# P times V as plain 32-bit matmuls on the two column halves of the array, and output-weight blocks staged in three tiles in turn

## The chip, the cores and the metric

The kernel runs on one core of one Trainium2 chip. The metric is the device time of one execution in microseconds (us), the median of several runs. The core has TensorE (PE), which multiplies a moving tile by a stationary one of up to 128 columns; VectorE (DVE), ScalarE (ACT) and GpSimd (POOL), which work on tiles; and SyncE (SP), whose queue issues the kernel's transfers. PE writes to PSUM, which DVE and ACT read.

## The reference

One layer of a hybrid backbone on 1024 latent tokens and 256 context tokens of width 1024, all in 32-bit floating point. The part that matters here, cut to its core:

```python
# 8 query heads in 2 groups of 4, one key/value head per group, head size 64,
# blocks of 128 queries; keys: the block, its two neighbours, and the context
s_loc = jnp.einsum('bnqhgd,bnkhd->bnhgqk', qb, kw) * scale
s_ctx = jnp.einsum('bnqhgd,bchd->bnhgqc', qb, kc) * scale
m = jnp.maximum(jnp.maximum(s_loc.max(-1), s_ctx.max(-1)), sk)
p_loc = jnp.exp(s_loc - m); p_ctx = jnp.exp(s_ctx - m)
inv = 1.0 / (p_loc.sum(-1) + p_ctx.sum(-1) + jnp.exp(sk - m))
o = (jnp.einsum('bnhgqk,bnkhd->bnqhgd', p_loc * inv, vw)
     + jnp.einsum('bnhgqc,bchd->bnqhgd', p_ctx * inv, vc))
...
mix_x = jnp.concatenate([att_x, ml_x], axis=-1) @ w_out
x = x + gt_m * rms_norm(mix_x, g_post_mix)
fx = swiglu(modulate(rms_norm(x, g_pre_ffn), sh_f, sc_f), w_ffn_in, w_ffn_out)
x = x + gt_f * rms_norm(fx, g_post_ffn)
```

Beside the attention, `ml_x` is a bidirectional mLSTM over chunks of 64 tokens. `att_x` and `ml_x` are 512 wide each; together they meet the output weight `w_out`.

## The kernel before

Most matmuls are split: a 32-bit operand is kept as a rounded part (type fp32r, "hi") and the remainder ("lo"), made by `split` (L64: ACT casts, L65: DVE subtracts), and the product is summed from two or three fp32r matmuls (`mm3`, L76 to L78, three). Plain 32-bit matmuls stand beside these: transposes (against an identity matrix), the mLSTM's L876 and L880, and L704, where the mLSTM's state step puts four matmuls of 64 stationary columns into the two halves of the PSUM partitions in turn.

The attention stage is a loop over 16 items, one for each block n of 128 queries and group g (item i has n = i // 2, g = i % 2). In item i:

- `Soft(i+2)`, for the item two later: scores per head (PE L972, L973), mask, sink and minimum (DVE L974), exponential (ACT L983), normalisation (POOL L988), into the tile `pr` (3 buffers).
- `Values(i)`: `tr(t)` transposes the probabilities of key tile t for four heads (L1002) into a PSUM bank `pt` (3 buffers) and splits them to `th` and `tl`; `mm(t)` multiplies by the values with L1012 (`th`) and L1013 (`tl`). The stationary tile `av2` has hi and lo of V side by side, 64 columns each, so the two halves of the result `po` must still be added: `out` copies one half (ACT L1020) and adds it to the other into `mix` (DVE L1021). A block has five key tiles, the first and the last block four: 76 in all.
- In items 0 to 7 the mLSTM of block i: scores (L862), two passes of values (L876 and L880; ACT L892, DVE L894 into `hs`), norm, output gate and transposes (L910, DVE L911). `hs` is loaded from DRAM by SP (L852).
- The output weight: eight blocks of 128 x 1024, each loaded raw into the one tile `wor` (`wout_raw(i)`, L926), and split at the letter `p` of the same item (ACT L938, POOL L939). `WSPLIT` says which block in which item (items 1, 2, 3, 5, 6, 7, 8, 9). The first three go to the tiles `woxh` and `woxl` and from there to DRAM (L921, in the next item), and are loaded again in items 8 and 9.

The strings `PLAN_ML` (items 0 to 7), `PLAN` (8 to 12) and `PLAN13` write out the order inside an item: T transposes, A scores, N exponentials, M products, O output, V, z, s, x mLSTM, p weight split. A scheduler moves instructions of independent work past each other on this basis; the end of the stage, from item 14 on, is a hand-written order (`manual_schedule`), in which the output projection (`omm`) is mixed with the last two items. The FFN follows.

Of the kernel before, what the change touches and what calls it, by code (L numbers as in the profile page):

```python
# [9 lines left out]
F32 = mybir.dt.float32  # L10
F32R = mybir.dt.float32r
# [3 lines left out]
ADD, SUB, MUL, MAX, MIN = ALU.add, ALU.subtract, ALU.mult, ALU.max, ALU.min  # L15

P = 128
D = 1024
KT = D // P
S = 1024  # L20
NT = S // P
L = 256
NC_ = L // P
# [8 lines left out]
VSIL, VCONV, VGML, VBADA, VGPM, VGPF = 0, 16, 28, 32, 64, 72  # L32
VID = 80
NVEC = VID + P
PLAN_ML = "T0 A0 A1 A2 A3 T1 T2 T3 M0 M1 T4 V0 N0 M2 M3 M4 O z V1 w s N1 x p l"
PLAN = "T0 A0 A1 A2 A3 T1 T2 T3 N0 M0 T4 M1 M2 N1 M3 M4 O z p l"
PLAN13 = "T0 A0 A1 A2 A3 m T1 T2 P0 T3 N0 M0 T4 M1 P1 M2 N1 M3 P2 M4 O P3 l"
WR = ((1, 2), (4, 5), (6, 7), (0, 3), (14, 15), (10, 13), (12, 8), (9, 11))
WTRIP = (3, 6, 7)
WLOADS = {8: (3, 6), 9: (7,)}  # L40
WSPLIT = {1: 3, 2: 6, 3: 7, 5: 0, 6: 4, 7: 1, 8: 2, 9: 5}


def body(tc, x, ctx, vecs, bcv, bada, gqm, gqf, wada, ws1, ws2, wt, wout, wfi, wfo,
         const, cosc, sinc, out):
    nc = tc.nc
    pe, act, dve, pool = nc.tensor, nc.scalar, nc.vector, nc.gpsimd
    dma = nc.sync.dma_start
# [13 lines left out]
    def split(hi, lo, raw):  # L62

        act.copy(hi, raw)  # L64
        dve.tensor_tensor(lo, raw, hi.bitcast(F32), SUB)  # L65
# [73 lines left out]
    vp = open_pool("V")  # L139
    V = vp[1].tile([P, NT, 4, 129], F32, name="V")  # L140
    Vc = vp[1].tile([P, NC_, 4, 129], F32, name="Vc")
    vp[1].tile([P, 88], F32, name="padv")
    av2 = vp[1].tile([P, NT + NC_, 4, 64], F32R, name="av2")
    G = vp[1].tile([P, 4, 16, 4], F32, name="G")
    pool.memset(V[:, :, :, 128:129], 1.0)
    pool.memset(G, 0.0)
# [6 lines left out]
    hl = [htp[1].tile([P, 4, S], F32R, name=f"hl{i}") for i in range(2)]  # L153
# [48 lines left out]
    pts = {}  # L202
# [94 lines left out]
    for sec in (1, 0):  # L297
        pr = [pa.tile([4, 512], F32, name=f"pr{sec}{i}", tag="mm", bufs=4) for i in range(2)]
        for kt in range(KT):
            w = R(8 + kt, f"wa{sec}_{kt}", (D,))  # L300
# [16 lines left out]
            for n, (k, a, b) in enumerate(ops):  # L317
                if late and n < 2:
                    prep_t(1, True, (n,))
                for i in range(2):  # L320
                    r = pe.matmul(pr[i], a[:, k, :], b[:, i * 512:(i + 1) * 512], start=kt == 0 and n == 0,
                                  stop=kt == KT - 1 and n == len(ops) - 1)
# [19 lines left out]
        r = act.copy(r4[:, 0:512], pr[0])  # L342
# [7 lines left out]
        for q in range(2):  # L350
            t = (hcol, scol)[sec][:, q]
# [36 lines left out]
    def vrow(i):  # L388
        return V[:, i] if i < NT else Vc[:, i - NT]

    def s1(i):
        ps = slab(i, 272, w1h, w1l)
        sf = i + 2 if i < NT else i - NT
        sb = 9 - i if i < NT else 1 - (i - NT)
        dve.tensor_tensor(G[:, 0:2, sf, :], ps[:, 0:8].rearrange("p (k h) -> p k h", h=4),
                          bcr[:, 0:8].rearrange("p (k h) -> p k h", h=4), ADD)
        dve.tensor_tensor(G[:, 2:4, sb, :], ps[:, 8:16].rearrange("p (k h) -> p k h", h=4),
                          bcr[:, 8:16].rearrange("p (k h) -> p k h", h=4), ADD)
        split(av2[:, i, 0::3], av2[:, i, 1:3], ps[:, 16:144].rearrange("p (g v) -> p g v", v=64))
        act.copy(vrow(i)[:, 0, 0:128], ps[:, 144:272])  # L400

    NI = NT + NC_
# [19 lines left out]
    for i in range(NI):  # L422
# [7 lines left out]
        if i == 0:  # L430
            r = st[:, 13:14]
# [7 lines left out]
        if i in (1, 2):  # L439
            b = i - 1  # L440
# [138 lines left out]
    def T(i, name):  # L579
        return q2.tile([P, S], F32, name=name, tag=f"s{i}")  # L580
# [134 lines left out]
    NIT = len(items)  # L715
    qhl, prs, wo, qlast = {}, {}, {}, [None]
# [23 lines left out]
    for j, name in enumerate(TILES):  # L740
# [4 lines left out]
        ps = tproj(j, name in ("mk0", "mk1", "ak"))  # L745
        i = int(name[-1]) if name[-1].isdigit() else 0
# [4 lines left out]
        elif name == "ak":  # L751
# [4 lines left out]
            th = T(0, "kth")  # L756
            for a, b, w, dst in ((kr, ks, S, slice(0, S)), (kc[:, 0:L], kc[:, L:2 * L], L, slice(S, S + L))):
                t = th[64:P] if w == S else kc[64:P, 2 * L:3 * L]
# [7 lines left out]
        elif name.startswith("aq"):  # L766
            t = T(0, f"aq{i}")
# [6 lines left out]
        else:  # L774
            t = R(14 if i == 3 else 15, "so", (S,))
# [26 lines left out]
        if 0 <= j - 3 < 9:  # L802
            s_ = j - 3
            if s_ >= 1 and s_ % 2 == 1:
                k = (s_ - 1) // 2
# [9 lines left out]
    pb = psB[1]  # L815
    mixp = open_pool("mix", side="right")
    mixt = mixp[1].tile([P, NT, 8, P], F32, name="mix")
    mix = [mixt[:, n] for n in range(NT)]
    atp = open_pool("att")
    qa = atp[1]  # L820
    for x_ in "hl":
        qa.tile([P, 4, P], F32R, name=f"t{x_}_", tag=f"pt{x_}", bufs=3)
    qa.tile([P, 80], F32, name="padq")
    for x_, n in (("pt", 3), ("po", 1)):
        pb.tile([P, 4, P], F32, name=x_, tag=x_, bufs=n)
# [88 lines left out]
    wraw = {}  # L914

    def wout_raw(i):

        j = WSPLIT.get(i - 1)
        if j in WTRIP:
            for d, t in zip(wo_d, wraw.pop(j)):  # L920
                dma(d[j], t.bitcast(F32))  # L921
        if i in WSPLIT:
            j = WSPLIT[i]
            wraw[j] = qa.tile([P, D], F32, name=f"wor{j}", tag="wor", bufs=1)
            with tc.issue_after(qlast[0]):
                dma(wraw[j], wout[j])  # L926

    def wout_tiles(j):
        return tuple(R(WR[j][p], f"wo{'hl'[p]}{j}", (D,), F32R) for p in range(2))
# [60 lines left out]
    class Values:  # L990
        def __init__(self, i):
            self.n, self.g = items[i]
            self.pr = prs.pop(i)
            self.kb0, _, self.nb = blocks(self.n)
            self.nt = self.nb + 2
            self.po = pb.tile([P, 4, P], F32, name="po", tag="po", bufs=1)
            self.p = {}

        def tr(self, t):
            pt = bank()  # L1000
            for h in range(4):
                pe.transpose(pt[:, h, :], self.pr[:, h, 1 + t * P:1 + (t + 1) * P], ident)  # L1002
            th = qa.tile([P, 4, P], F32R, name="th_", tag="pth", bufs=3)
            tl = qa.tile([P, 4, P], F32R, name="tl_", tag="ptl", bufs=3)
            split(th, tl, pt)
            self.p[t] = th, tl

        def mm(self, t):
            vt = self.kb0 + t if t < self.nb else NT + t - self.nb
            v2 = av2[:, vt, 2 * self.g:2 * self.g + 2].rearrange("p a v -> p (a v)")  # L1010
            th, tl = self.p.pop(t)
            pe.matmul(self.po, v2, th, start=t == 0, stop=False)  # L1012
            pe.matmul(self.po, v2, tl, start=False, stop=t == self.nt - 1)  # L1013

        def out(self):

            g = self.g
            rg, ot = slice(g * 64, g * 64 + 64), slice(64 - g * 64, P - g * 64)
            o2 = qa.tile([P, 4, P], F32, name="o2", tag="o2", bufs=1)
            act.copy(o2[rg], self.po[ot])  # L1020
            dve.tensor_tensor(mix[self.n][rg, 0:4, :], self.po[rg], o2[rg], ADD)  # L1021

    tc.keep_in_program_order(act.preload_act_table_set("natural_log_exp_and_others"))
    ml_load(0)
    for i in range(2):
        a = Soft(i)
# [14 lines left out]
    def omm(n, hf, ks):  # L1041

        h, l = mhl[n, hf]
        first, last = (0, 7) if n == 0 else (4, 3)
        for k in ks:
            j = 4 * hf + k
            for i in range(2):
                sl = slice(i * 512, (i + 1) * 512)
                mm3(ops_[n][:, sl], (h[:, k], l[:, k]), (wo[j][0][:, sl], wo[j][1][:, sl]), j == first, j == last)


    for i in range(NIT):
        a = Soft(i + 2) if i + 2 < NIT else None
        b = Values(i)
        if i + 3 < NIT:
            q_load(i + 3)
        if i == NIT - 2:
            break
        wout_raw(i)
        for k in (PLAN_ML if i < NT else PLAN13 if i == NIT - 3 else PLAN).split():  # L1060
            op, n = k[0], int(k[1:] or 0)
            if op == "w" and i + 1 < NT:
                ml_load(i + 1)
            elif op == "T" and n < b.nt:
                b.tr(n)
            elif op == "M" and n < b.nt:
                b.mm(n)
            elif op == "O":
                b.out()
            elif op == "A" and a:  # L1070
                a.scores(n)
            elif op == "N" and a:
                a.norm(n)
            elif op == "V" and i < NT:
                ml_values(i, n)
            elif op == "x" and i < NT:
                ml_norm(i)
            elif op == "s" and i + 1 < NT:
                ml_scores(i + 1)
            elif op == "z" and 1 <= i <= NT:  # L1080
                ml_out(i - 1)
            elif op == "l":
                for j in WLOADS.get(i, ()):
                    wout_load(j)
            elif op == "p" and i in WSPLIT:
                wout_split(i)
            elif op == "m":
                msplit(0, 0)
                ops_[0] = pb.tile([P, 1024], F32, name="op", tag="s", bufs=2)
            elif op == "P":  # L1090
                omm(0, 0, range(n, n + 1))
# [1 line left out]

    order = tc.manual_schedule()
    order.__enter__()
    def mm_t(b, *ts):
        for t in ts:
            b.mm(t)

    msplit(0, 1)  # L1100
    b.tr(0)
    b.tr(1)
    b.tr(2)
    omm(0, 1, range(1))
    mm_t(b, 0, 1)
    b.tr(3)
    omm(0, 1, range(1, 2))
    mm_t(b, 2, 3)
    b2 = Values(NIT - 1)
    b2.tr(0)  # L1110
    b.out()
    b2.tr(1)
    omm(0, 1, range(2, 3))
    b2.tr(2)
    msplit(1, 1)
    act.preload_act_table_set("sqrt_and_others")
    mm_t(b2, 0, 1)
    b2.tr(3)
    omm(0, 1, range(3, 4))
    mm_t(b2, 2, 3)  # L1120
    ops_[1] = pb.tile([P, 1024], F32, name="op", tag="s", bufs=2)
    omm(1, 1, range(4))
    b2.out()
    order.__exit__(None, None, None)
    close(atp)
    close(aqp)
# [165 lines left out]
    th = {}  # L1292
# [73 lines left out]
    N1 = NT - 1  # L1366
# [359 lines left out]
    for p in range(4, HT):  # L1726
        j = p - 5
# [40 lines left out]
        else:  # L1768
            X4 += two_banks()
            t = pb.tile([P, D], F32, name="fx2", tag="s", bufs=2)  # L1770
# [97 lines left out]
    for s_ in range(1, 8):  # L1868
        q0 = (s_ - 1) * NJ
        KL = 4 if s_ == 7 else 2  # L1870
        if s_ == 2:
            t = pb.tile([P, D], F32, name="fy0", tag="s", bufs=2)
# [120 lines left out]
```

## Time and profile before

| what | value |
|---|---|
| median of 3 runs | 1188.93 us (1188.78 to 1191.32) |
| the profiled execution's own time | 1189.32 us |
| its span | 1187.5 us, 16397 instructions |
| granted TensorE clock | 0.998 |
| attention stage | 297 to 467.5 us of the span |
| the last items' outputs (L1020) | items 13, 14, 15 at 454.3, 460.8, 466.7 us |

The profile is one execution, taken by the hardware profiler. A row of the timeline gives the start in us, the duration in us, the engine, the line, the operation, and output <- inputs with their shapes; for PE the used rows and columns of the array stand ahead of the shape of the moving operand. "x4" at its end means four such instructions in a row, and the duration is then from the first one's start to the last one's end. A row of the windows gives a stretch (from:to), its length, and each engine's busy time with its number of instructions, then the granted clock, the transfer engines' busy share and GB/s. A row of the waits gives who waited for what: us in total, times, the longest. Matmuls are pipelined, so the duration of one is longer than the distance to the next.

### The profile page before, as it was taken

The numbers are of one execution on the slowest core, as the hardware profiler recorded it, in microseconds if no ns is written. First come the engines' busy times: TensorE is split into PE (matmuls) and PEld (weight loads), VectorE is DVE, ScalarE is ACT, GpSimd is POOL, SyncE is SP. The second block draws the span as 40 slices with busy tenths as digits, with TensorE's granted clock in tenths as the row PEclk, the third lists the DMA queues.
The fourth block names the chain that finished last, engine by engine and source line by source line (L and its number), as shares of the span: only waits on it lengthen the run. The fifth ranks groups of instructions, "written<-read, shape, count | busy, mean of one in ns | idle before, by whom it ended". The sixth has DMA issues, their size and how long they took to land.

```text
span 1187.5 us, 16397 instructions
## 1 busy us (share of the span) xinstructions
PE 1164.6 (98%) x5881; PEld 964.5 (81%) x5881; DVE 818.3 (69%) x1437; ACT 578.1 (49%) x1075; POOL 152.8 (13%) x204
## 2 busy tenths in 40 slices
PE   9899999999999989999999999999999999999997
PEld 3799888877888877888788888888888888888886
DVE  5864768863989984468767767776777656544566
ACT  6743442222877885777533334333333335434543
POOL 1550001225544550000000000000000000000000
PEclk9999999999999999999999999999999999999999
DMA  9522955648886713321242675656553557665853
GB/s 367 196 72 64 376 191 168 186 132 245 207 223 162 220 38 99 150 91 52 87 142 97 218 241 200 216 202 221 204 182 123 191 186 269 201 220 181 310 186 124
DMA packets 101992, 214.89 MB, mean 181 GB/s; under 512 B 10004, under 2 KB 39316, under 8 KB 100504
## 3 DMA queue, kind: packets, MB, share of 16 engines
q1 hardware_dynamic: 101912, 213.85, 54.4%
q8 instruction: 46, 0.75, 0.3%
q14 instruction: 34, 0.28, 0.1%
HBM read 157.19 MB, written 55.97 MB: 179 GB/s over the span
## 4 chain that ended last, share of the span: by engine, by line
PE 82%; DVE 10%; DMA 3%; ACT 2%; issue 2%; POOL 1%; SPq 0%; DVEq 0%; ACTq 0%; POOLq 0%
PE xv L78 8%; PE xv L76 8%; PE xv L77 8%; PE pt L78 6%; PE pt L76 6%; PE pt L77 6%; PE t L596 3%; PE t L595 2%; PE t L598 2%; PE op L78 2%; PE op L76 2%; PE op L77 2%; PE fx L76 2%; PE fx L78 2%; PE fx L77 2%
## 5 line engine op out<-in xcount | busy, mean ns | idle before, releaser
L65 DVE TENSOR_TENSOR fo<-fr,fo 128x1024 fp32r<-128x1024 f32 x77 | 92.7, 1222 | 70.9 <-ACT fo L64 70.6
L64 ACT CAST fo<-fr 128x1024 fp32r<-128x1024 f32 x77 | 79.7, 1052 | 73.9 <-PE pt L78 33.2
L595 PE MATMUL t<-hh,th 128*128 128x512 f32 x208 | 82.4, 396 | 0.0
L596 PE MATMUL t<-hl,th 128*128 128x512 f32 x208 | 81.7, 393 | 0.0
L1399 ACT CAST wS<-wr 128x512 fp32r<-128x512 f32 x88 | 54.2, 623 | 55.2 <-PE pt L78 36.6
L1401 DVE TENSOR_TENSOR wS<-wr,wS 128x512 fp32r<-128x512 f32 x88 | 60.4, 688 | 19.8 <-ACT wS L1399 19.7
L76 PE MATMUL xv<-tT,wS 128*128 128x512 f32 x168 | 65.6, 391 | 0.0
L78 PE MATMUL xv<-tT,wS 128*128 128x512 f32 x168 | 65.6, 391 | 0.0
L598 PE MATMUL t<-hh,tl 128*128 128x512 f32 x208 | 65.6, 393 | 0.0
L77 PE MATMUL xv<-tT,wS 128*128 128x512 f32 x168 | 65.5, 390 | 0.0
L76 PE MATMUL op<-woh,mh 128*128 128x512 f32 x128 | 51.0, 398 | 0.0
L77 PE MATMUL op<-wol,mh 128*128 128x512 f32 x128 | 50.0, 391 | 0.0
L78 PE MATMUL op<-woh,ml 128*128 128x512 f32 x128 | 50.0, 390 | 0.0
L1147 DVE TENSOR_TENSOR wr<-wr 128x512 f32<-128x512 f32 x66 | 45.5, 690 | 1.4
L1433 ACT ACTIVATE es<-es 128x512 f32<-128x512 f32 x22 | 13.9, 632 | 66.5 <-DVE es L1150 66.5
L595 PEld LDWEIGHTS t<-hh,th 128*128 128x128 f32 x208 | 39.1, 188 | 8.3 <-issue 0.3
L596 PEld LDWEIGHTS t<-hl,th 128*128 128x128 f32 x208 | 39.1, 188 | 7.8 <-issue 0.8
L598 PEld LDWEIGHTS t<-hh,tl 128*128 128x128 f32 x208 | 37.4, 188 | 6.9 <-issue 0.5
L76 PE MATMUL pt<-fo 128*128 128x512 f32 x110 | 42.8, 389 | 0.0
L77 PE MATMUL pt<-fo 128*128 128x512 f32 x110 | 42.8, 389 | 0.0
L78 PE MATMUL pt<-fo 128*128 128x512 f32 x110 | 42.8, 389 | 0.0
L972 PE MATMUL s<-k,qh 128*128 128x256 f32 (+1 forms) x128 | 40.5, 327 | 0.9 <-DVE sm L974 0.8
(1016 smaller groups left out, 3403.1 us busy)
## 6 DMA issues: line engine op xcount, KB each, us to landing
wr<-in_wfi SPq DMA_DIRECT2D x44, 512.0 KB, 4.8
wb<-in_wada SPq DMA_DIRECT2D x24, 512.0 KB, 5.8
s_d<-a SPq DMA_DIRECT2D x22, 512.0 KB, 6.8
bt<-in_wfo SPq DMA_DIRECT2D x44, 256.0 KB, 4.0
tb_d<-bt SPq DMA_DIRECT2D x11, 1024.0 KB, 3.9
fr<-s_d SPq DMA_DIRECT2D x44, 256.0 KB, 4.4
fr<-tb_d SPq DMA_DIRECT2D x44, 256.0 KB, 4.3
fr<-a_d SPq DMA_DIRECT2D x33, 256.0 KB, 4.5
```

What stands on the lines that cost most here:

```text
L64: act.copy(hi, raw)
L65: dve.tensor_tensor(lo, raw, hi.bitcast(F32), SUB)
L76: pe.matmul(ps, a[0], b[0], start=first, stop=False, **kw)
L77: pe.matmul(ps, a[0], b[1], start=False, stop=False, **kw)
L78: pe.matmul(ps, a[1], b[0], start=False, stop=last, **kw)
L595: pe.matmul(o, wh[:, kt], m[0], start=f, stop=False)
L596: pe.matmul(o, wh[:, kt], m[1], start=False, stop=False)
L598: pe.matmul(o, wl[:, kt], m[0], start=False, stop=l)
L972: pe.matmul(o, qh[:, h, :], k2[g][:, kc], start=True, stop=False)
L1147: dve.tensor_tensor(out, a, b, SUB)
L1399: act.copy(w[:, 0], raw)
L1401: dve.tensor_tensor(w[:, 1], raw, w[:, 0].bitcast(F32), SUB)
```

## The change

V stays plain 32-bit (`av`, 64 columns a group), copied by ACT in the first stage in place of its split. `tr(t)` makes one copy of the transposed probabilities, on ACT for even t and on DVE for odd t, into a plain tile `ts` with 9 buffers (`NTS`). The products of both groups of a block are made together in the odd item: `pv` takes the key tiles in reverse, and for each gives two plain matmuls with 64 stationary columns, group 1 into partitions 64 to 127 of `po` and group 0 into 0 to 63, in a pinned order; M0 is key tiles 0 to 2, M1 3 and 4. One ACT copy (`pv_out`) brings the block to `mix`; there is no add. The plans become pairs for even and odd items.

The raw output-weight blocks for items 1 to 3 are requested as before; from item 4 on the block of item i + 1 is requested in item i, and these five go through the tiles `wor`, `woxh` and `woxl` in turn.

```diff
-            th = qa.tile([P, 4, P], F32R, name="th_", tag="pth", bufs=3)
-            tl = qa.tile([P, 4, P], F32R, name="tl_", tag="ptl", bufs=3)
-            split(th, tl, pt)
-            self.p[t] = th, tl
-
-        def mm(self, t):
-            vt = self.kb0 + t if t < self.nb else NT + t - self.nb
-            v2 = av2[:, vt, 2 * self.g:2 * self.g + 2].rearrange("p a v -> p (a v)")
-            th, tl = self.p.pop(t)
-            pe.matmul(self.po, v2, th, start=t == 0, stop=False)
-            pe.matmul(self.po, v2, tl, start=False, stop=t == self.nt - 1)
-
-        def out(self):
...
-            act.copy(o2[rg], self.po[ot])
-            dve.tensor_tensor(mix[self.n][rg, 0:4, :], self.po[rg], o2[rg], ADD)
+            self.p[t] = ts = qa.tile([P, 4, P], F32, name="ts_", tag="pts", bufs=NTS)
+            if t % 2:
+                dve.tensor_copy(ts, pt)
+            else:
+                act.copy(ts, pt)
+
+    pos = {}
+
+    def pv(a, b, ts, more, pin=True):
+
+        ts = [t for t in ts if t < a.nt][::-1]
+        first = a.n not in pos
+        if first:
+            pos[a.n] = pb.tile([P, 4, P], F32, name="po", tag="po", bufs=1)
+        for t in ts:
+            vt = a.kb0 + t if t < a.nb else NT + t - a.nb
+            for g, x_ in ((1, b), (0, a)):
+                r = pe.matmul(pos[a.n][64 * g:64 * g + 64], av[:, vt, g], x_.p.pop(t), start=first and t == ts[0],
+                              stop=not more and t == ts[-1])
+                if pin and (t != ts[0] or not g):
+                    tc.keep_in_program_order(r)
+
+    def pv_out(n):
+        act.copy(mix[n][:, 0:4, :], pos.pop(n))
...
-        if i in WSPLIT:
-            j = WSPLIT[i]
-            wraw[j] = qa.tile([P, D], F32, name=f"wor{j}", tag="wor", bufs=1)
-            with tc.issue_after(qlast[0]):
-                dma(wraw[j], wout[j])
+        for k in [i] if i < 4 else [i + 1]:
+            if k in WSPLIT:
+                j = WSPLIT[k]
+                wraw[j] = qa.tile([P, D], F32, name=f"wor{j}", tag=("wor", "woxh", "woxl")[max(k - 5, 0) % 3], bufs=1)
+                with tc.issue_after(qlast[0]):
+                    dma(wraw[j], wout[j])
...
-PLAN_ML = "T0 A0 A1 A2 A3 T1 T2 T3 M0 M1 T4 V0 N0 M2 M3 M4 O z V1 w s N1 x p l"
+PLAN_ML = ("T0 A0 A1 A2 A3 T1 T2 T3 V0 N0 T4 z V1 w s N1 x p l", "T0 A0 A1 A2 A3 T1 T2 V0 N0 T3 M0 T4 z V1 w s M1 O N1 x p l")
...
-            elif op == "M" and n < b.nt:
-                b.mm(n)
-            elif op == "O":
-                b.out()
+            elif op == "M" and i % 2:
+                pv(b0, b, ((0, 1, 2), (3, 4))[n], not n)
+            elif op == "O" and i % 2:
+                pv_out(b.n)
```

In the hand-written end, item 14's products wait for item 15's: `pv(b, b2, range(4))` stands after the last transpose `b2.tr(3)` and the split of the mLSTM half of block 1's row (`msplit(1, 1)`), ahead of `omm(0, 1, range(3, 4))`.

On PE, the part of the program's order in item 5 before the change, where L1012 and L1013 are the products with `th` and `tl`:

```order
L1012 MATMUL po<-th__3745,av_91 128x512
L1002 MATMUL pt<-vec,pr__3364 128x128 x12
L1013 MATMUL po<-tl__3746,av_91 128x512
L1012 MATMUL po<-th__3778,av_91 128x512
L1013 MATMUL po<-tl__3779,av_91 128x512
L1002 MATMUL pt<-vec,pr__3364 128x128 x4
L1012 MATMUL po<-th__3787,av_91 128x512
L876 MATMUL pt<-cs_2367,qz_2970 128x129 x2
```

After the change, in the same item (L1020 is now the line of the products):

```order
L880 MATMUL pt<-V,wl_3595 128x129 x2
L1020 MATMUL po<-ts__3683,av 64x512
L1020 MATMUL po<-ts__3528,av 64x512
L1002 MATMUL pt<-vec,pr__3299 128x128 x4
L1020 MATMUL po<-ts__3676,av 64x512
L1020 MATMUL po<-ts__3521,av 64x512
L1020 MATMUL po<-ts__3645,av 64x512
L1020 MATMUL po<-ts__3490,av 64x512
L1002 MATMUL pt<-vec,pr__3299 128x128 x4
```

The products come in pairs, group 1 ahead of group 0, and other plain matmuls (transposes, mLSTM) stand between the groups of pairs; fp32r matmuls no longer stand there.

On SP, around the load of `hs` for item 5, before:

```order
L921 DMA wo_dh<-woxh_3545 128x1024
L850 DMA qz_2742<-q_dr 64x2x128
L921 DMA wo_dl<-woxl_3546 128x1024
L926 DMA wor_3738<-in_wout 128x1024
L724 DMA qh<-aq_dh 64x4x128 x2
L850 DMA qz_2742<-q_dr 64x2x128
L852 DMA hs_3700<-so_d 128x4x128
```

And after:

```order
L921 DMA wo_dh<-woxh_3468 128x1024
L850 DMA qz_2731<-q_dr 64x2x128 x2
L921 DMA wo_dl<-woxl_3469 128x1024
L927 DMA wor_3483<-in_wout 128x1024
L927 DMA wor_3638<-in_wout 128x1024
L927 DMA wor_3809<-in_wout 128x1024
L852 DMA hs_3601<-so_d 128x4x128
```

Three raw loads (L927, the blocks split in items 5, 6 and 7) now follow the last store from `woxl` back to back, where one stood before; the second goes into the tile `woxh` and the third into `woxl`, which those stores read.

More of the change, by code (lines that the diff above doesn't have):

```diff
@@ L34 @@
 NVEC = VID + P
-PLAN_ML = "T0 A0 A1 A2 A3 T1 T2 T3 M0 M1 T4 V0 N0 M2 M3 M4 O z V1 w s N1 x p l"
-PLAN = "T0 A0 A1 A2 A3 T1 T2 T3 N0 M0 T4 M1 M2 N1 M3 M4 O z p l"
-PLAN13 = "T0 A0 A1 A2 A3 m T1 T2 P0 T3 N0 M0 T4 M1 P1 M2 N1 M3 P2 M4 O P3 l"
+PLAN_ML = ("T0 A0 A1 A2 A3 T1 T2 T3 V0 N0 T4 z V1 w s N1 x p l", "T0 A0 A1 A2 A3 T1 T2 V0 N0 T3 M0 T4 z V1 w s M1 O N1 x p l")
+PLAN = ("T0 A0 A1 A2 A3 T1 T2 T3 N0 T4 N1 z p l", "T0 A0 A1 A2 A3 T1 T2 T3 N0 M0 T4 N1 M1 O z p l")
+PLAN13 = "T0 A0 A1 A2 A3 m T1 T2 P0 T3 N0 M0 T4 P1 N1 P2 M1 O P3 l"
+NTS = 9
 WR = ((1, 2), (4, 5), (6, 7), (0, 3), (14, 15), (10, 13), (12, 8), (9, 11))
@@ L142, in body @@
     vp[1].tile([P, 88], F32, name="padv")
-    av2 = vp[1].tile([P, NT + NC_, 4, 64], F32R, name="av2")
+    av = vp[1].tile([P, NT + NC_, 2, 64], F32, name="av")
     G = vp[1].tile([P, 4, 16, 4], F32, name="G")
@@ L398, in s1 @@
                           bcr[:, 8:16].rearrange("p (k h) -> p k h", h=4), ADD)
-        split(av2[:, i, 0::3], av2[:, i, 1:3], ps[:, 16:144].rearrange("p (g v) -> p g v", v=64))
+        act.copy(av[:, i], ps[:, 16:144].rearrange("p (g v) -> p g v", v=64))
         act.copy(vrow(i)[:, 0, 0:128], ps[:, 144:272])
@@ L820, in body @@
     qa = atp[1]
-    for x_ in "hl":
-        qa.tile([P, 4, P], F32R, name=f"t{x_}_", tag=f"pt{x_}", bufs=3)
+    qa.tile([P, 4, P], F32, name="ts_", tag="pts", bufs=NTS)
     qa.tile([P, 80], F32, name="padq")
@@ L995, in __init__ @@
             self.nt = self.nb + 2
-            self.po = pb.tile([P, 4, P], F32, name="po", tag="po", bufs=1)
             self.p = {}
@@ L1002, in tr @@
                 pe.transpose(pt[:, h, :], self.pr[:, h, 1 + t * P:1 + (t + 1) * P], ident)
-            th = qa.tile([P, 4, P], F32R, name="th_", tag="pth", bufs=3)
-            tl = qa.tile([P, 4, P], F32R, name="tl_", tag="ptl", bufs=3)
-            split(th, tl, pt)
-            self.p[t] = th, tl
-        def mm(self, t):
-            vt = self.kb0 + t if t < self.nb else NT + t - self.nb
-            v2 = av2[:, vt, 2 * self.g:2 * self.g + 2].rearrange("p a v -> p (a v)")
-            th, tl = self.p.pop(t)
-            pe.matmul(self.po, v2, th, start=t == 0, stop=False)
-            pe.matmul(self.po, v2, tl, start=False, stop=t == self.nt - 1)
-        def out(self):
-            g = self.g
-            rg, ot = slice(g * 64, g * 64 + 64), slice(64 - g * 64, P - g * 64)
-            o2 = qa.tile([P, 4, P], F32, name="o2", tag="o2", bufs=1)
-            act.copy(o2[rg], self.po[ot])
-            dve.tensor_tensor(mix[self.n][rg, 0:4, :], self.po[rg], o2[rg], ADD)
+            self.p[t] = ts = qa.tile([P, 4, P], F32, name="ts_", tag="pts", bufs=NTS)
[18 more added lines that the diff above has]
+        act.copy(mix[n][:, 0:4, :], pos.pop(n))
     tc.keep_in_program_order(act.preload_act_table_set("natural_log_exp_and_others"))
@@ L1049, in omm @@
                 mm3(ops_[n][:, sl], (h[:, k], l[:, k]), (wo[j][0][:, sl], wo[j][1][:, sl]), j == first, j == last)
+    b = None
     for i in range(NIT):
         a = Soft(i + 2) if i + 2 < NIT else None
-        b = Values(i)
+        b0, b = b, Values(i)
         if i + 3 < NIT:
@@ L1059, in body @@
         wout_raw(i)
-        for k in (PLAN_ML if i < NT else PLAN13 if i == NIT - 3 else PLAN).split():
+        for k in (PLAN_ML[i % 2] if i < NT else PLAN13 if i == NIT - 3 else PLAN[i % 2]).split():
             op, n = k[0], int(k[1:] or 0)
@@ L1095, in body @@
     order.__enter__()
-    def mm_t(b, *ts):
-        for t in ts:
-            b.mm(t)
     msplit(0, 1)
@@ L1104, in body @@
     omm(0, 1, range(1))
-    mm_t(b, 0, 1)
     b.tr(3)
-    omm(0, 1, range(1, 2))
-    mm_t(b, 2, 3)
     b2 = Values(NIT - 1)
     b2.tr(0)
-    b.out()
+    omm(0, 1, range(1, 2))
     b2.tr(1)
+    b2.tr(2)
     omm(0, 1, range(2, 3))
-    b2.tr(2)
+    b2.tr(3)
     msplit(1, 1)
     act.preload_act_table_set("sqrt_and_others")
-    mm_t(b2, 0, 1)
-    b2.tr(3)
+    pv(b, b2, range(4), False, False)
     omm(0, 1, range(3, 4))
-    mm_t(b2, 2, 3)
     ops_[1] = pb.tile([P, 1024], F32, name="op", tag="s", bufs=2)
     omm(1, 1, range(4))
-    b2.out()
+    pv_out(b.n)
     order.__exit__(None, None, None)
```

## The prediction

> **What bounds the kernel now.** I read the page's busy shares first, then the stretches of the attention stage, then TensorE's waits in it.
>
> ```profile
> PE 1164.6 (98%) x5881; PEld 964.5 (81%) x5881; DVE 818.3 (69%) x1437; ACT 578.1 (49%) x1075; POOL 152.8 (13%) x204
> core 0: us, PE busy (x) PEld busy (x) DVE busy (x) ACT busy (x) POOL busy (x), PEclk, DMA share, GB/s
> 297.00:467.50 170.50, 161.68 (x1093) 140.01 (x1092) 144.13 (x398) 132.73 (x341) 78.54 (x93) 1.00 0.58 154
> 336.20:361.70 25.50, 25.10 (x183) 22.05 (x182) 23.12 (x71) 20.71 (x60) 14.24 (x16) 1.00 0.98 255
> 410.80:430.80 20.00, 16.07 (x105) 13.73 (x103) 16.05 (x36) 15.98 (x33) 12.24 (x13) 1.00 0.46 122
> 430.80:444.70 13.90, 12.85 (x83) 10.93 (x84) 13.56 (x33) 12.66 (x30) 5.88 (x10) 1.00 0.00 1
> 467.50:1187.50 720.00, 713.91 (x3173) 589.08 (x3171) 477.62 (x664) 324.26 (x528) 0.96 (x1) 1.00 0.52 180
> ```
>
> TensorE (PE) is busy for 98% of the span. The stretch 297 to 467.5 us is the attention stage; behind it PE is busy for 713.91 of 720 us, so microseconds won or lost in the stage reach the end. In the stage PE is idle for 170.50 − 161.68 = 8.8 us, and more than these 8.8 us cannot be won by taking waits away. Items 3 and 4 (336.2 to 361.7) leave 0.4 us of them; items 8 and 9 (410.8 to 430.8) leave 3.9; items 10 and 11 leave 1.05, and there VectorE (DVE) is the fullest engine, with 13.56 of 13.9.
>
> ```profile
> engine line waited for: us in total, times, longest us
> PE po L1012 <- ACT th__4450 L64: 2.1, 1, 2.1
> PE po L1012 <- ACT th__4560 L64: 1.5, 1, 1.5
> PE pt L1002 <- DVE hs L894: 1.3, 3, 0.5
> PE pt L1002 <- DVE tl__4645 L65: 0.6, 1, 0.6
> PE pt L876 <- ACT hs L892: 0.6, 1, 0.6
> 412.71 0.58 ACT L64 CAST th__4441<-pt 128x512 fp32r<-128x512 f32 x1
> 415.56 1.04 ACT L938 CAST woh<-wor 128x1024 fp32r<-128x1024 f32 x1 [2.27 <-DMA wor<-in_wout]
> 416.51 0.58 ACT L64 CAST th__4450<-pt 128x512 fp32r<-128x512 f32 x1
> ```
>
> The first rows are PE's waits in the stage, the last three ScalarE's (ACT) timeline. Both big waits, 3.6 us together, are behind the raw output-weight block: ACT stands 2.27 us for the transfer into `wor`, and the cast that PE needs is queued behind it. The other 5.2 us are small: a third of them hang on the mLSTM (`hs`), others on the split of the transposed probabilities.
>
> **Term 1, the products on the array.** Before, 76 tiles take two fp32r matmuls each. After, the same 76 are plain 32-bit matmuls on 64 columns, and the trace has each plain one as two instructions: L876 is written 8 × 2 × 4 = 64 times and counts 128.
>
> ```profile
> L876 PE MATMUL pt<-cs,qz 128*128 128x129 f32 x128 | 20.1, 279 | 0.6 <-ACT hs L892 0.6
> 382.50 0.61 PE L876 MATMUL pt<-cs,qz 128*128 128x129 f32 x4
> 443.78 0.49 PE L1002 MATMUL pt<-vec,pr__4596 128*128 128x128 f32 x3
> 444.35 0.39 PE L77 MATMUL op<-wol,mh 128*128 128x512 f32 x1
> 444.58 0.40 PE L78 MATMUL op<-woh,ml 128*128 128x512 f32 x1
> 6.03 1.88 PE L321 MATMUL pr<-wa,cz 128*4 128x512 f32 x4
> 206.41 0.39 PE L598 MATMUL t<-hh,tl 128*128 128x512 f32 x1
> 206.72 0.33 PE L704 MATMUL pu<-V,mkc 128*64 128x129 f32 x2
> 206.72 0.44 PE L704 MATMUL pu<-V,mkc 128*64 128x129 f32 x4
> 206.72 1.10 PE L704 MATMUL pu<-V,mkc 128*64 128x129 f32 x16
> 208.09 0.39 PE L595 MATMUL t<-hh,th 128*128 128x512 f32 x1
> ```
>
> One fp32r matmul of 512 columns follows another after 0.23 us (444.35 to 444.58): before, 152 × 0.23 = 35.0 us. A plain one of 512 columns takes 0.43 us an instruction ((1.88 − 0.59 for the last one's tail) / 3). If the halves did nothing for each other, 152 × 0.43 = 65.4 us; if they run side by side, 0.215 an instruction, 32.7.
>
> L704 is the only place that uses column halves, four matmuls a step, halves in turn. Its three rows are one group, seen up to 206.85, up to 206.90 and whole: each further pair of instructions adds 0.11 us (0.33, 0.44, ... 1.10), where plain instructions of 129 columns on the full array take 0.11 each too ((0.61 − 0.28) / 3 at L876), one source matmul per 0.22. So the halves do overlap: one source matmul per 0.11. But there is a price at the group's edges. From the start of the L598 ahead to that of L595 are 1.68 us; less two fp32r matmuls (0.46) and eight times 0.11 (0.87) leaves 0.35. I read it so: the two instructions of one matmul share a half and run one after the other, in order; the other half starts when the second does. So n matmuls take n + 1 slots, not n: the first slot and the last have one half empty. One slot of 0.11 is that; the other 0.24 is getting in (206.72 is 0.31 behind 206.41, not 0.23; the first weights are exposed) and out. At 512 columns the empty slot is 0.43 and the 0.24 stays, since it is weight loading and switching.
>
> In the changed order the 76 matmuls stand in 18 groups (three each in items 1, 3, 5, two each in 7, 9, 11, 13, one in the tail), cut by transposes and mLSTM matmuls. So they take (76 + 18) × 0.43 + 18 × 0.24 = 40.4 + 4.3 = 44.7 us: **+9.7** against 35.0. Bounds: without the empty slot growing, 32.7 + 18 × 0.35 = 39.0, **+4.0**; with no edge at all −2.3; with no overlap 65.4 + 4.3, +34.7. A change of number format elsewhere in the stage costs next to nothing: from the first of three transposes (443.78) past one fp32r matmul to L77 (444.35) are 0.57 us, of which 3 × 0.11 + 0.23 = 0.56 are work. So the fewer such changes save nothing.
>
> "TensorE: Matmul & The Clock Gate" of the Trainium skill (Part 3, Measured speedup vs the span model) has a pack of matmuls on different tiles last one matmul and about 4 ns for each further tile; an empty slot is not in it. By that the sum would lose 18 × 0.43 = 7.7 us. The trace's 0.35 us at a group of 129 columns is more than such a pack allows, but no run here shows it at 512.
>
> **Term 2, the raw blocks.** From item 4 on each is requested one item earlier.
>
> ```profile
> 410.17 0.55 SPq L926 DMA_DIRECT2D wor<-in_wout  x1
> wor<-in_wout SPq DMA_DIRECT2D x3, 512.0 KB, 6.9
> ```
>
> The request at 410.17 was used at 415.56; an item here is about 10 us, so a request an item ahead lands in time: both waits go, **−3.6**. What is late next there is PE itself: 16.07 of the remaining 16.4 us, against ACT's 15.98 and DVE's 16.05, which both shrink in term 3.
>
> **Term 3, the splits.**
>
> ```profile
> 297.00:467.50 170.50, 45.18 (x79) 1.00 0.58 154
> 297.00:467.50 170.50, 53.46 (x79) 1.00 0.58 154
> L1436 ACT COPY ev<-xv 128x512 f32<-128x512 f32 x21 | 12.4, 589 | 40.2 <-PE xv L78 40.2
> L346 DVE COPY Vc<-pr 4x512 f32<-4x512 f32 x2 | 1.4, 675 | 0.1
> ```
>
> The first two rows are L64 (ACT) and L65 (DVE) in the stage, 76 of 79 of them probability tiles, 0.57 and 0.68 us each. 76 casts and 76 subtracts become 76 copies, 44 on ACT (even tiles) at 0.589 and 32 on DVE at 0.675; 16 adds and 8 of 16 output copies go too. DVE loses about 41 us of 144, ACT about 22 of 133. Only the waits of PE count: of 5.2 us between 0 (mLSTM, scores) and all, middle **−2.6**. The split of V, gone from the front, hung behind no wait of PE that the waits show there: 0.
>
> Products of two items now stand in the odd item. In an even one PE has about 12.6 − 2.3 = 10.3 us, DVE about 8.9 and ACT 8.7, so PE stays the fullest: 0. In items 10 to 14 the margin is gone (PE 4.1, ACT 4.6 in an even item); up to +1.5 over three, taken as 0 since three buffers of probabilities even it out.
>
> **Term 4, new waits.** Three raw loads stand in a row ahead of the `hs` load of item 5 in SP's queue; the second and third reuse staging tiles and wait for the stores out of them.
>
> ```profile
> 358.46 0.55 SPq L921 DMA_DIRECT2D wo_dh<-woxh  x1
> 360.55 0.33 SPq L921 DMA_DIRECT2D wo_dl<-woxl  x1
> 363.63 0.55 SPq L852 DMA_DIRECT2D hs<-so_d  x1
> wo_dl<-woxl SPq DMA_DIRECT2D x3, 512.0 KB, 4.3
> hs<-so_d SPq DMA_DIRECT2D x2, 256.0 KB, 6.7
> 373.08 1.14 ACT L892 ACTIVATE hs<-pt,dn 128x128 f32<-128x128 f32 x4 [0.36 <-issue]
> ```
>
> The store of 360.55 lands 4.3 us on, at 364.9; with two further issues `hs` goes out at about 366, 2.4 us later than 363.63. From landing (363.63 + 6.7 = 370.3) to use at 373.08 are 2.8 us of slack, so little may be left over; if the loads also share the transfer engines with it (0.98 busy in that stretch), up to 4.3. I take **+1.0**, bounds 0 and +4.3. Behind the waiting ACT instruction stand the copies that PE's products need. In the tail all products wait for the last copy, one of 0.59 less the weights' split beside it: **+0.4**, bounds 0 and 0.6.
>
> **Sum:** 9.7 − 3.6 − 2.6 + 1.0 + 0.4 = +4.9 against the profiled run's 1189.32 us: 1194.2. The median lies 0.39 lower: **1193.8**.
>
> **Rivals.** About 0.2% (2.4 us) is what a measurement here can tell from no change: faster is below 1186.5, slower above 1191.3.
> - The empty slot doesn't grow with the columns, or is hidden (term 1 between −2.3 and +4.0; the whole sum between −7.1 and −0.8): 1181.8 to 1188.1, the middle 1186. This ends on the other side. For it: eight slots explain most of L704's row. Against: 0.35 us must go somewhere. It decides if a slot is under about 0.15 us (−2.8 + 18 slots = 0). The span model of the Trainium skill that term 1 names would come out in this rival.
> - The relief is larger: all 5.2 us of small waits go and nothing new comes, term 1 as forecast: 9.7 − 3.6 − 5.2 = +0.9, 1189.8. For it: DVE 41 us lighter; against: a third of the waits aren't its.
> - `hs` is late in full, or bunching bites: +3.3 and +1.5, 1197 to 1198.6.
> - The halves don't run together at 512 columns, so that the change does not do what it says: 34.7 in place of 9.7, and at best all 8.8 us of idle go, or the other terms hold: +25.9 to +29.9, 1215 to 1219. For it: no 512-column row; against: L704.
>
> **Chances.** Forecast (own range 1190.5 to 1197) 0.58, of it 0.50 slower and 0.08 same; empty slot small 0.20 (faster 0.12, same 0.08); larger relief 0.08 (same); late `hs` 0.09 and halves apart 0.05 (slower). Faster 0.12, same 0.24, slower 0.64. The range, 1185.5 to 1198.6, leaves out the halves apart and the lower part of the small slot.
>
> **What would show it.** In the changed profile: a group of four source matmuls of 512 columns lasts about 5 × 0.43 + tail (right), 4 × 0.43 (slot hidden) or 8 × 0.43 (no overlap); PE's instruction groups in the stage add up to 9.7 us more; ACT never waits for a `wor` transfer; PE's waits on L64 and L65 are gone; `hs` of item 5 is issued behind three raw loads and L892 waits under 2 us. The forecast is wrong if the stage isn't longer than 170.5 us.

## The result and the profile after

The changed kernel takes 1181.64 us (median of 4 runs, 1181.29 to 1181.65) against 1190.12 us (1188.78 to 1191.89) of the kernel before: ratio 0.9928, 95% interval 0.9915 to 0.9941. It is 8.5 us faster, where the prediction had 1193.8 us, slower.

The page of the changed kernel, then its windows: the attention stage, and its two halves (items 0 to 7, items 8 to 15). The same output-projection matmul ends the stage in both kernels, at 466.54 us before and at 458.90 after, so the stage 297 to 467.50 is now 297 to 459.86, 7.64 us shorter.

```profile
span 1179.9 us, 16215 instructions
PE 1161.8 (98%) x5881; PEld 947.8 (80%) x5881; DVE 781.5 (66%) x1367; ACT 557.7 (47%) x1035; POOL 153.9 (13%) x204
core 0: us, PE busy (x) PEld busy (x) DVE busy (x) ACT busy (x) POOL busy (x), PEclk, DMA share, GB/s
297.00:459.86 162.86, 158.62 (x1101) 123.26 (x1102) 108.78 (x341) 113.43 (x303) 78.24 (x93) 1.00 0.62 176
297.00:398.86 101.86, 98.85 (x730) 80.01 (x731) 77.78 (x266) 73.89 (x218) 52.25 (x62) 1.00 0.77 211
398.86:459.86 61.00, 59.77 (x373) 43.25 (x372) 31.00 (x75) 39.54 (x87) 25.99 (x32) 1.00 0.36 116
```

And the same halves of the kernel before:

```profile
297.00:398.70 101.70, 98.64 (x712) 87.31 (x711) 92.35 (x285) 82.25 (x232) 51.20 (x61) 1.00 0.75 190
398.70:467.50 68.80, 63.04 (x384) 52.69 (x382) 51.79 (x114) 50.48 (x109) 27.34 (x33) 1.00 0.34 102
```

VectorE is 35 us lighter in the stage (144.13 to 108.78), ScalarE 19 (132.73 to 113.43). By the clock the first halves end at nearly the same time (398.70, 398.86), but not at the same place of the work. At 398.70 the kernel before has still 16 instructions of the mLSTM's passes of values to run (L876 and L880, 0.11 us each), which lie ahead of the cut in the changed kernel; that one has three score matmuls more behind the cut. So somewhat over 1 us of the gain, by this estimate, was made in items 0 to 7. Most of it is from items 8 to 15, where PE's idle time falls from 5.8 to 1.2 us. In the whole stage it falls by 4.6 us, from 8.8 to 4.2, and PE's busy time by 3.1.

TensorE's waits in the changed stage:

```profile
PE po L1020 <- DVE ts__4746 L1005: 0.8, 1, 0.8
PE pt L910 <- ACT ts__3567 L1007: 0.8, 1, 0.8
PE pt L910 <- ACT ts__3893 L1007: 0.8, 1, 0.8
PE pt L910 <- ACT ts__3233 L1007: 0.5, 1, 0.5
PE s L974 <- DMA ql<-aq_dl: 0.5, 1, 0.5
PE pt L910 <- DVE ts__4174 L1005: 0.4, 1, 0.4
```

Of the old ones only small waits for `pr` and `sm` are left, 0.3 us each: there is no wait for `mix` or `hs`, and `th` and `tl` exist no more. The new ones are the mLSTM's transposes (L910), which wait for a PSUM bank that a copy of probabilities has still to read (2.5 us), the tail's products, which wait for the last copy (0.8), and one score matmul, which waits for a transfer (0.5).

The products themselves, in item 5 of the changed kernel (PE's timeline; L1020, with `ts__36..` of group 1 and `ts__35..` of group 0):

```profile
365.77 0.61 PE L880 MATMUL pt<-V,wl 128*128 128x129 f32 x4
366.31 0.64 PE L1020 MATMUL po<-ts__3683,av 128*64 128x512 f32 x1
366.32 0.64 PE L1020 MATMUL po<-ts__3528,av 128*64 128x512 f32 x1
366.79 0.59 PE L1020 MATMUL po<-ts__3683,av 128*64 128x512 f32 x1
366.80 0.59 PE L1020 MATMUL po<-ts__3528,av 128*64 128x512 f32 x1
367.32 0.66 PE L1002 MATMUL pt<-vec,pr__3299 128*128 128x128 f32 x4
```

There is no empty slot. In the program the matmul of `ts__3683` stands ahead of that of `ts__3528`, and each is two instructions. On the chip the first one of group 0 starts 0.01 us behind the first one of group 1, ahead of group 1's second. Two matmuls take two slots of 0.43. From the end of L880's work (365.77 + 4 × 0.11 = 366.21) to the transposes at 367.32 are 1.11 us, 0.86 of them the slots: the edges are 0.25, as forecast (0.24). The trace has the 18 groups that were forecast, and none has an empty slot: a group of four key tiles, the largest, lasts 3.58 us from its first start to the next instruction's (453.82 to 457.40), eight slots of 0.43 and 0.14.

### The profile page after: what moved, and what is told of

It is laid out like the page before. It is cut to its first block, busy times and chain, and to the rows that moved or that the text cites. A ratio compares the mean times of both kernels' runs of the same rounds, so it can differ in the third digit from the quotient of the medians.

```text
span 1179.9 us, 16215 instructions
## 1 busy us (share of the span) xinstructions
PE 1161.8 (98%) x5881; PEld 947.8 (80%) x5881; DVE 781.5 (66%) x1367; ACT 557.7 (47%) x1035; POOL 153.9 (13%) x204
## 4 chain that ended last, share of the span: by engine, by line
PE 89%; DVE 4%; DMA 4%; ACT 1%; issue 1%; SPq 0%; POOL 0%; DVEq 0%; ACTq 0%
PE xv L79 8%; PE xv L78 8%; PE xv L77 8%; PE pt L79 6%; PE pt L77 6%; PE pt L78 6%; PE po L1020 3%; PE t L597 3%; PE t L596 3%; PE t L599 3%; PE pt L1002 3%; PE op L77 3%; PE op L79 2%; PE op L78 2%; PE fx L77 2%; PE slab L77 2%
## 5 line engine op out<-in xcount | busy, mean ns | idle before, releaser
L66 DVE TENSOR_TENSOR fo<-fr,fo 128x1024 fp32r<-128x1024 f32 x77 | 92.9, 1223 | 70.2 <-ACT fo L65 68.4
```

## The experiments

Times are medians. The kernel before ran beside each group of runs, on the same chip, and took 1190.41 to 1190.95 us.

### What the early raw requests are worth

`e1_late_raw` puts the old requests back into the changed kernel:

```diff
-        for k in [i] if i < 4 else [i + 1]:
-            if k in WSPLIT:
...
+        if i in WSPLIT:
+            j = WSPLIT[i]
+            wraw[j] = qa.tile([P, D], F32, name=f"wor{j}", tag="wor", bufs=1)
```

> The changed kernel with the raw output-weight blocks requested as before the change (in the item that splits them, one tile). The theory that the two big waits of ScalarE for the raw block were worth what TensorE stood behind them (2.13 and 1.5 us): those waits are back and the time is about 3.6 us above the changed kernel's 1181.6, near 1185.3. Rival: with the products taken late, TensorE no longer stands behind the casts, so the early request is worth nothing and the time stays within 1 us of 1181.6.

Measured: 1181.0 us. It was repeated beside the changed kernel (`e16_late_raw_again`, `e15_after_again`):

> The changed kernel with the raw blocks requested late, once more beside the changed kernel: if the early request is worth nothing there, within 0.8 us of the changed kernel.

> The changed kernel once more on this chip, for comparison with the two runs beside it: 1181.6 within 1.

Measured: 1181.72 us (1180.97 to 1182.09) late, 1181.36 (1179.91 to 1182.16) early. In the changed kernel the early request is worth nothing that can be measured. The waits of the repeated run, ScalarE's for the block and TensorE's largest:

```profile
ACT woh L938 <- DMA wor<-in_wout: 2.6, 2, 2.3
PE po L1019 <- DVE ts__4746 L1004: 0.8, 1, 0.8
PE pt L1001 <- ACT ts__4361 L1006: 0.8, 1, 0.8
```

ScalarE stands for one block as long as before (2.3 us, up to 409.57), but TensorE shows no idle time behind that: the products that it runs from 407.60 on read copies that were done by 407.28. The 0.8 us of the last row stand behind the next block's cast, whose own wait is 0.3; those of the row above are the tail's, which the changed kernel has too. The other way round, `e2_early_raw` gives the kernel before the new requests alone (the loop over `k` in the change's diff, and nothing else of it):

> The kernel before the change with the early requests alone. If the two waits are worth 3.6 us on their own: about 1186.5 against 1190.1 before. If the 3.6 us need the lighter engines too (VectorE and ScalarE are nearly full in items 8 and 9): between 1187.5 and 1190.

Measured: 1186.98 us (1185.98 to 1187.52), 3.4 us below its 1190.41. So the 3.6 us of the forecast were right for the old order, and are gone in the new one whether the request is early or not.

### The halves of the array

`e3_halves_apart` writes the products of a group of key tiles first for group 1, then for group 0:

```diff
-        for t in ts:
-            vt = a.kb0 + t if t < a.nb else NT + t - a.nb
-            for g, x_ in ((1, b), (0, a)):
+        for g, x_ in ((1, b), (0, a)):
+            for t in ts:
+                vt = a.kb0 + t if t < a.nb else NT + t - a.nb
```

> The changed kernel, with the products of a group of key tiles written for group 1 first and then for group 0, so that equal halves stand next to each other in the program. If TensorE runs the halves side by side only where they are neighbours, most of 33 us of overlap is lost: 1205 to 1215. If an instruction for the free half can pass several that wait for the other half, the time stays within 2 us of 1181.6.

Measured: 1189.39 us (1188.63 to 1190.76), 7.8 us above the changed kernel: between the two expectations. Three key tiles at once, in item 7 (`ts__40..`, `ts__3975` are group 1, in program order first; `ts__38..` group 0):

```profile
392.81 1.07 PE L1020 MATMUL po<-ts__4013,av 128*64 128x512 f32 x2
393.72 0.59 PE L1020 MATMUL po<-ts__4006,av 128*64 128x512 f32 x1
393.73 0.64 PE L1020 MATMUL po<-ts__3854,av 128*64 128x512 f32 x1
394.15 0.59 PE L1020 MATMUL po<-ts__4006,av 128*64 128x512 f32 x1
394.21 0.59 PE L1020 MATMUL po<-ts__3854,av 128*64 128x512 f32 x1
...
395.50 1.02 PE L1020 MATMUL po<-ts__3816,av 128*64 128x512 f32 x2
```

Group 1 has six instructions, then group 0 six. The first two run alone. With the third (393.72) group 0's first one starts, 0.01 us behind: it passes the three of group 1 that still wait. One slot earlier four were waiting, and it did not start. The two instructions by which it began late run alone at the end. So eight slots in place of six; with two key tiles, where three wait from the start, nothing is lost.

`e4_one_group` makes all products of a block in one group, which stands where the second group stood, with ten buffers; for the room two unused pad tiles are dropped:

```diff
-                pv(b0, b, ((0, 1, 2), (3, 4))[n], not n)
+                pv(b0, b, (0, 1, 2, 3, 4), False)
```

> The changed kernel with all products of a block in one group (M0 takes all key tiles, ten buffers of copies, two unused pad tiles dropped): 8 groups in place of 18. If a group costs 0.25 us at its edges and no empty slot: 10 groups fewer give -2.5 us, near 1179.1. If a group cost an empty slot of 0.43 us more: -6.8 us, near 1174.8. If later products make new waits, slower than 1181.6.

Measured: 1188.11 us (1186.71 to 1188.78), 6.5 us slower than the changed kernel. Ten groups fewer did not show in the time. There are new waits: TensorE stood 3.9 us for `hs` before L908, and 0.8 us three times for a copy. That the later products made them is the likely reading; no run separates it. The time does not give the edge's price, but the trace has the edge unchanged: a group of five key tiles lasts 4.44 us from its first start to the next instruction's, ten slots of 0.43 and 0.14.

### What the lighter engines are worth

Five runs load VectorE, ScalarE or both in the changed kernel again, with a copy into a tile that nobody reads behind each copy of probabilities (in `e12_dve_half` behind those of the even key tiles alone); two of them copy the probabilities, three a constant tile:

```diff
+            jk = qa.tile([P, 4, P], mybir.dt.bfloat16, name="jk_", tag="jk", bufs=1)
+            dve.tensor_copy(jk, ts)
...
+            dve.tensor_copy(jk, av[:, 0:4].rearrange("p a g v -> p a (g v)"))
```

> The changed kernel with one more VectorE copy for each of the 76 copies of probabilities, into a tile that nobody reads, so that VectorE is loaded again nearly as before (some 25 to 45 us more in the stage). If the small waits went because VectorE is lighter: they come back, 1184 to 1187. If they went because the products are taken late and no longer stand behind a split just made: within 1 us of 1181.6.

> The same extra copy on VectorE and one more on ScalarE for each of the 76 (two unused pad tiles dropped to make room). ScalarE and VectorE are then as full as before the change or fuller. Lighter engines as the cause: 1187 to 1191. Late products as the cause: within 2 us of 1181.6.

> The changed kernel with one more VectorE copy per key tile (76) from a tile that is constant in this stage, so that it waits for nothing. If VectorE's time was what cost 13.8 us in the run with copies of the probabilities: again 1192 to 1196. If it was that VectorE then stood waiting for ScalarE's copies: 1181.6 to 1186.

> The same constant copy, for the even key tiles only (44). If the cost grows with VectorE's load: between the changed kernel and the run with 76, about 1187. If VectorE only counts once it is nearly full: within 2 us of 1181.6.

> The constant copy on ScalarE instead of VectorE (76). If ScalarE's lightness was part of the gain: 1185 or more. If only VectorE's was: within 2 us of 1181.6.

Measured: 1195.42 us with VectorE's copy of the probabilities, 1195.47 with ScalarE's beside it; 1201.95 with 76 constant copies on VectorE, 1195.04 with 44, and 1188.97 with 76 on ScalarE. No load is free: with VectorE at its old load (92.9 us busy up to 398.8 with copies of the probabilities, 92.5 before the change) the changed order is slower than the kernel before. Late products are no cover for a loaded engine: TensorE then waits for other work of it. The largest wait of that run is for the score reduction:

```profile
PE s L973 <- DVE sm L975: 6.0, 7, 2.1
```

The size of these costs is no clean price of VectorE's time. A copy of the probabilities waits for the copy that it reads, and VectorE with it. The constant copies wait for nothing, and the scheduler put them early: 40 of the 44 start before 347 us and 68 of the 76 before 384, so that up to about 347 both runs load VectorE alike, and half the copies are no test of half the load. The granted clock fell too, as the windows show (76 constant copies, then 44):

```profile
297.00:398.80 101.80, 87.75 (x593) 69.87 (x594) 95.73 (x284) 61.36 (x178) 44.58 (x51) 0.93 0.66 183
297.00:398.80 101.80, 91.95 (x649) 75.73 (x650) 87.59 (x273) 66.06 (x189) 46.97 (x53) 0.95 0.69 190
```

The cleaner test is the other way: VectorE lightened in the old order. `e13_no_lo` and `e14_early_raw_no_lo` take the subtract out of `tr` in the kernel before. They leave out the low part of the probabilities; the second product reads the high part again, so that TensorE's work stays the same:

```diff
-            split(th, tl, pt)
-            self.p[t] = th, tl
+            act.copy(th, pt)
+            self.p[t] = th, th
```

> The kernel before without VectorE's 76 subtracts (leaves out the low part of the probabilities: the second product reads the high part again, so TensorE's work is the same). VectorE 52 us lighter in the old order. If lighter engines alone give the gain: the splits' waits (2.1 us, up to 5.2) go and the raw block's stay or shrink, 1183 to 1187.5. If the gain needs the late products: 1189 to 1190.5.

> The same with the early raw requests. Lighter engines alone: about 3 us below the run without the subtracts or the sum of both, 1181 to 1184. Late products needed: as the early requests alone, 1187.

Measured: 1183.69 us (1182.13 to 1184.63) without the subtract, and 1180.31 (1179.85 to 1180.60) with the early requests as well, against 1190.71 before and 1181.36 for the changed kernel on the same chip. Without the subtract the old order is 7.0 us faster, and the requests give 3.4 on top. The subtract's absence does three things at once: VectorE is busy for 43 us less (818.3 to 775.4 us of the span), the second product no longer waits for a subtract, and the bank `pt` comes free as soon as the cast has read it. No run separates these. Where a good part of the 7.0 comes from, by the window of the run without the subtract:

```profile
297.00:398.80 101.80, 101.25 (x749) 92.80 (x750) 73.85 (x258) 85.02 (x244) 53.35 (x64) 1.00 0.79 201
```

In the same 101.8 us TensorE now gets through 749 instructions, 36 more than before (713 in the same stretch), and idles for 0.55 us; before it idled for about 3.

### Copies and their places

`e6_t4_dve` copies key tile 4 on VectorE (`if t % 2 or t == 4`), `e9_act_more` copies tile 1 on ScalarE (`if t == 3`), and `e7_z_late` puts the mLSTM's transposes behind V1 (`T4 V1 z w s`):

> The changed kernel with the copy of key tile 4 on VectorE in place of ScalarE. The new waits of TensorE are before the mLSTM's transposes (L910) for a bank that a copy on ScalarE still reads (0.8, 0.8, 0.5 us); if the copy is late because it stands behind ScalarE's exponentials, they go: 1179.5. If any copy there is late: no change.

> The changed kernel with the copies of key tile 1 on ScalarE too, so that VectorE keeps only key tile 3's (16 of 32 copies move). If VectorE's load is what counts: VectorE 11 us lighter, 1178 to 1181. If copies on ScalarE come late behind the exponentials: 1183 to 1186.

> The changed kernel with the mLSTM's transposes (z) behind the second pass of values (V1) in the plan, not ahead of it. If the waits before L910 (2.9 us with edges) only come from where z stands: they go, about 1179. If another instruction then waits for the same bank: no change, or slower by as much.

Measured: 1184.3, 1181.87 and 1182.43 us. None is better than the changed kernel's 1181.64 and 1181.36. In the first the waits on ScalarE's copies before L910 are gone as meant, and 2.1 us of waits for VectorE's score reduction (L975) came in their place, with 0.6 more for the transfer of `ql`; in the second VectorE is lighter (100.02 us up to 459.86) and the time is the same. No version tried that computes the whole layer is faster than the changed kernel by more than the runs scatter.

## Why the prediction was wrong, point by point

**Term 1 failed, in one step: that the two instructions of one matmul "run one after the other, in order; the other half starts when the second does", so that n matmuls take n + 1 slots.** The slot was read out of the 0.35 us at the edges of L704 and scaled to 0.43 us at 512 columns. The trace has n slots: 76 × 0.43 + 18 × 0.25 = 37.2 us, +2.2 against 35.0 and not +9.7. This is the first rival. The trace agrees there with the span model of the Trainium skill ("TensorE: Matmul & The Clock Gate", Part 3, Measured speedup vs the span model): the two tiles of a pair start 0.01 us apart and no slot is empty. L704's rows could have told it: they show 0.33 us for two instructions and 0.44 for four. Two instructions that share a half and run one after the other would have added 0.11 between the first and the second.

With +2.2 in term 1 and the rest as forecast the sum is −2.6, 1186.3 us: faster, near the middle of that rival, and still 4.7 us above what was measured. That the rival's low end (1181.8) is where the kernel came out is luck, since that end has no edges at all, and the edges are there. The other 4.7 us are the business of the terms on the waits.

**Term 2** (−3.6) was right as a price: −3.4 in the old order. As a term of this sum it was not its own: the new order of products takes the same waits away. It is the order and not the lighter VectorE that does so, since without the subtract the requests were still worth 3.4 in the old order. ScalarE, which is lighter too, was not tested apart there. Taken together, the requests and the new order remove these waits once.

**Term 3** (−2.6, at most −5.2) was too small and its bound false. "More than these 8.8 us cannot be won by taking waits away" failed: the run without the subtract and with early requests won 10.4 us with the same matmuls. PE's idle time is not all its waiting. The kernel before, that run and the changed kernel, each from just behind the last matmul ahead of the scores to the end of the stage, 1118 of PE's instructions in all three:

```profile
292.70:467.50 174.80, 165.21 (x1118) 142.90 (x1117) 147.37 (x407) 137.00 (x348) 81.64 (x102) 1.00 0.59 158
293.59:458.77 165.18, 161.06 (x1118) 143.78 (x1117) 102.60 (x331) 135.62 (x348) 82.21 (x104) 1.00 0.62 166
293.56:459.86 166.30, 161.30 (x1118) 125.41 (x1117) 111.27 (x347) 116.84 (x308) 81.26 (x102) 1.00 0.62 177
```

In the second row the stretch is 9.6 us shorter than in the first, and PE's idle time in it only 5.5 (9.6 to 4.1). The other 4.1 us come out of what counts as PE's busy time, with the same matmuls. How a wait hides there, in the kernel before:

```profile
353.00 0.28 PE L972 MATMUL s<-k,qh 128*128 128x256 f32 x1
353.12 0.28 PE L973 MATMUL s<-k,ql 128*128 128x256 f32 x1
353.39 0.50 PE L1012 MATMUL po<-th__3566,av 128*128 128x512 f32 x1
355.59 0.40 PE L1012 MATMUL po<-th__3599,av 128*128 128x512 f32 x1
356.13 0.51 PE L1013 MATMUL po<-tl__3600,av 128*128 128x512 f32 x1
```

Such a score matmul is followed by the next after 0.12 us, but the product of `th__3566`, which waited for ScalarE's cast, came 0.27 after the last one, with no idle time shown: the tail of 0.28 that the profile reckons for the last one covers the wait of 0.15. The product of `tl__3600` waited for VectorE's subtract. It came 0.54 after the one ahead of it, where 0.23 is usual between two such products, and of these 0.31 the tail covers 0.17. Several waits on a split were of this size. So the term is the waits by distance between starts, not by idle time, and by the run without the subtract it is worth 7.0 us in the old order, not 2.6.

**Term 4:** `hs` was no wait. The three raw loads did stand in a row ahead of it, as SP's rows of the changed kernel show:

```profile
357.17 3.21 SPq L927 DMA_DIRECT2D wor<-in_wout  x3
360.47 0.39 SPq L852 DMA_DIRECT2D hs<-so_d  x1
```

The three took 3.21 us to issue, but the stores ahead of them were earlier too, and `hs` landed in time (median 3.6 us, where it was 6.2). The tail's wait was forecast at 0.4 and measured 0.8. Not foreseen were the waits of L910 for a bank, 2.5 us, and that of a score matmul for a transfer, 0.5.

The pieces do not add up by themselves: measured, −7.0 for the subtract and −3.4 for the requests, both in the old order, +2.2 for the products, and +3.8 for the new waits (L910, the tail, the transfer) make −4.4, and the kernel won 8.5 to 9.4 us. What the change saves beyond the subtract (16 adds, half the output copies, ScalarE's 19 us) and the waits on the mLSTM and the scores that are gone lie in that difference; no run separates them. Taken as a whole the account does close. Over the same 1118 instructions the changed kernel is 8.5 us shorter (174.80 to 166.30) with 2.2 more for its products, so its waits, the new ones included, are 10.7 us fewer; the run without the subtract and with early requests lost 9.6 us of waits in that stretch. So the order with plain products rids TensorE of as much waiting as taking the subtracts and the late requests away does in the old order. Which part of the change removed which wait stays open.

## What to carry to other kernels

Where an engine's pipelined instructions overlap, count its waits by the distance between starts, not by idle time: the tail hides a wait or a part of it, and so the subtracts of a nearly full VectorE were worth 7 us to a TensorE that looked 95% busy in the stage. An edge read from a short instruction is to be taken apart before it is scaled to a long one. And two remedies for one wait are worth one of them: price each in the order that the other leaves behind.

## What the runs showed of the hardware

- An instruction for one column half starts ahead of instructions for the other half that stand before it in the program: in `e3_halves_apart`, ahead of three, not of four. With key tiles paired the 64-column halves of 512 columns run side by side without loss (0.43 us for two instructions); with six instructions for one half ahead of six for the other, two slots of eight are lost, and the kernel is 7.8 us slower.
- The granted clock was lower in some stretches with waits, but the idle share alone does not fix it. Over the 102 us up to 398.8, with TensorE idle for 14% it was 0.93 (76 constant copies on VectorE); with 8% it was 0.98 in one run (76 on ScalarE) and 1.00 in another (copies of the probabilities on both); with 3%, in the kernel before, 1.00.
